# Low parts of 40 weight tiles of layer 1 formed during layer 0, kept in DRAM and loaded

## The chip, the cores and the metric

The program runs on one core of a Trainium2 chip, with TensorE (PE), VectorE (DVE), ScalarE (ACT), GpSimd (POOL) and SyncE (SP), which issues most of the transfers. The metric is the device time of one execution in microseconds (us).

## The reference

A trunk of two layers works on 256 latent and 256 context tokens of width 1024, in fp32. Each layer does the following:

```
h  = rms_norm(x, g) * (1 + scale) + shift            # scale, shift, gates: silu(c) @ w_ada
p  = h @ w_in                                        # one projection, split in columns
A  = bidirectional chunked gated delta rule on q, k, v of p, then norm and silu(z)
B  = b * dwconv3(c * h')                             # short gated convolution
C  = 2-D neighbourhood attention, with all context keys in the same softmax
y  = (gA * (A @ w_pa) + gB * (B @ w_pb) + gC * (C @ w_pc)) @ w_o     # sigmoid gates from p
x += gate1 * y
x += gate2 * ((silu(a) * b) @ w_down),  a, b = dwconv3(h2 @ w_up)
```

Context and latent tokens share the weights. In layer 1 (the last) the context is needed only for keys, values and the delta state, so most projections there have 256 columns instead of 512. The result is the normalized latent stream.

## The kernel before

**Products in three passes.** The matmuls that carry the weights work on operands that are rounded to the fp32r type. To keep fp32 accuracy each operand is held as a high part (the rounded value) and a low part (value minus high part), and `mm3` (L172) adds hi x hi, hi x lo and lo x hi: a tile of 1024 x 128 weights costs 8 x 3 = 24 matmuls. With 512 columns the text calls it a wide tile, with 256 a narrow one.

**Splitting a weight tile.** `wsplit` (L148) loads a tile of 128 x 1024 values (512 KB) on SP's queue into a ring of three raw buffers (tag `wraw`), takes `whi` and `wlo` from rings of three (layer 0) or four (layer 1), casts the raw values into `whi` on ACT (L162) and subtracts on DVE or POOL into `wlo` (L165). Every nth subtraction goes to POOL; n is `LOE`, by stage: in layer 1 every 4th in the delta stage, every 2nd in the rest of the short convolution and z, every 3rd in attention, every 2nd later. A raw buffer is free when the subtraction is done, a `whi` or `wlo` slot when the matmuls of its tile are.

**Order of a layer.** Norm with the first two k tiles and the small a/b projection pipelined into it; then the delta stage: the projections of k, v and q (`gproj`, L509), gram matrices, a substitution of 30 serial steps on DVE (L684 to L688: one product and one addition each), transposes and small matmuls (L735 to L745), and a scan over eight steps into which the matmuls of the short convolution are interleaved (`fill`, L782); the rest of the short convolution, z and the output norm; attention in four head pairs (L978); the merge of the three branches (L1080); w_o; the up projection (22 steps of two tiles, L1174); the down projection (eight tiles of 22 slices, loaded in three pieces, L1203). The modulation vectors of later stages are products on DVE (`ada_all`, L225): each step loads 512 KB into a ring of two and makes one or two passes (L241); `ada_to` spreads 80 steps over layer 0's merge, up and down projection.

**Who sets the order.** The kernel's text gives a program order, and a planner with its own costs places each instruction in its engine's sequence when its inputs and buffers are there in the plan; some matmuls are pinned to program order. On the chip each engine, and SP's and POOL's queues, work through their sequences in order. Temporaries come from rings: `tmp` with tag `tmp` (three) and `tg` (two).

The lines that the change touches:

Of the kernel before, what the change touches and what calls it, by code (L numbers as in the profile page):

```python
# [9 lines left out]
F32 = mybir.dt.float32  # L10
F32R = mybir.dt.float32r
AF = mybir.ActivationFunctionType
ALU = mybir.AluOpType
# [47 lines left out]
PRE = (12, 13, 14, 15, 20, 21)  # L61

ADT = (0, 32, 16, 32)

CTO, CTD = (2, 0), 1
NC0, NUP, HLE = 4, 2, 0
# [15 lines left out]
def trunk(ctx, tc, xin, cin, cbin, con, par, w_ad0, w_ada, w_in, w_ab, bias, w_p, w_o, w_up, w_dn, out, dbg=None):  # L82
# [62 lines left out]

    cb, wsp = [], []

    def wsplit(src, k, m=128, pool=None, bufs=None, dst=None):  # L148
        raw = wraw(src.rearrange("p a b -> p (a b)"), k * m, "wr").rearrange("p (a b) -> p a b", b=m)
        if pool is None:  # L150
            pool, bufs = wsp[0]
        if dst is not None:
            hi, lo = dst
        else:
            hi = pool.tile([P, 8, 128], F32R, tag="whi", bufs=bufs, name="whi")[:, :k, :m]
            lo = pool.tile([P, 8, 128], F32R, tag="wlo", bufs=bufs, name="wlo")[:, :k, :m]
        lo_n[0] += 1
        E_ = G if lo_every[0] and lo_n[0] % lo_every[0] == 0 else V
        na, nb = cuts[0] if k == KD and m == P else (1, 1)
        for i in range(na):  # L160
            c = slice(i * k // na, (i + 1) * k // na)
            A.copy(hi[:, c], raw[:, c])  # L162
        for i in range(nb):
            c = slice(i * k // nb, (i + 1) * k // nb)
            E_.tensor_tensor(lo[:, c], raw[:, c], hi[:, c].bitcast(F32), ALU.subtract)  # L165
        return hi, lo
# [88 lines left out]
    def ada_to(n):  # L255

        if not ada_on:
            ada_on.append(1)
            next(ada_gen)
        while ada_at[0] < n:  # L260
            next(ada_gen)
            ada_at[0] += 1
# [105 lines left out]
    for l in range(L):  # L368
# [15 lines left out]

        adf = {}

        def before(q):
            if l == 0:
                if q == 0:
                    adf[0] = ada_first(0, a0p)  # L390
                    next(adf[0])
                next(adf[q])
                if q == 3:
                    nc.sync.dma_start(cb[0], cbin)
                    A.activation(cb[0], cb[0], AF.Silu)
                if q < 3:
                    adf[q + 1] = ada_first(q + 1, a0p)
                    next(adf[q + 1])
            if q == QW[l]:
                raw = wraw(w_ab[l].rearrange("p a b -> p (a b)"), KD * 16, "wr").rearrange("p (a b) -> p a b", b=16)  # L400
                A.copy(wab[:, :, 0:16], raw)
                V.tensor_tensor(wab[:, :, 16:32], raw, wab[:, :, 0:16].bitcast(F32), ALU.subtract)
                for i in range(NT[l]):
                    pre[GK + i] = wsplit(w_in[l, GK + i], KD)
            if q == QX and l == 0:
                for i in range(NT[l], NT[l] + NPX):
                    pre[PRE[i]] = wsplit(w_in[l, PRE[i]], KD, pool=s0p, bufs=NPX)


        first = {}  # L410
# [55 lines left out]
        def proj(ti, n, name="prj", bank=pbank):  # L466
            if ti in first:
                return first.pop(ti)
            w = pre.pop(ti) if ti in pre else wsplit(w_in[l, ti], KD)
            ps = bank(name)  # L470
            mm3(ps[:, : n.stop - n.start], w, hh, hl, KD, n, True, True)
            return ps
# [279 lines left out]

        def short_conv():
            def fproj(ti):
                hi, lo = wsplit(w_in[l, ti], KD)
                ps = pbank("prj")
                for k in range(KD):
                    for i, (a, b) in enumerate(((hi, hh), (hi, hl), (lo, hh))):
                        mm = PE.matmul(ps[:, OW], a[:, k, :], b[:, k, NA_], start=k == 0 and i == 0, stop=k == KD - 1 and i == 2)  # L759
                        if in_scan[0]:  # L760
                            tc.keep_in_program_order(mm)
                        yield ps
# [214 lines left out]
        with left("at", l) as at:  # L977
            for i in range(4):  # L978
# [23 lines left out]
                if i % 2 == 0:  # L1002
# [3 lines left out]

                    vst = [wp.tile([P, 2, 4, P], F32R, tag="araw", bufs=2, name="vst") for _ in range(2)]
                    for a in range(2):
                        wsplit(w_in[l, NV + i + a], KD, dst=(vh[:, a], vl[:, a]))
                    for b in range(4):  # L1010
                        ps = pbank("pv")
                        n = slice(b * P, b * P + P)
# [67 lines left out]
        for j in range(KD):  # L1080
            acc = tmp("acc")
            for bi, br in enumerate(BRO):
# [12 lines left out]
                    V.tensor_tensor(acc[:, OW], acc[:, OW], gt, ALU.add)  # L1095
                if l == 0:
                    ada_to(ADT[0] + (3 * j + bi + 1) * ADT[1] // 24)
            split(mh[:, j], ml[:, j], acc[:, OW])
        RX.close()

# [50 lines left out]
        with right("f", l) as fp:  # L1151
# [22 lines left out]
            for i in range(FT):  # L1174
# [13 lines left out]
                split(fh[:, i], fl[:, i], uv[0])  # L1188
                if not last:
                    ada_to(sum(ADT[:2]) + (i + 1) * ADT[2] // FT)  # L1190
            cut = 0 if last else CTD
            stat = Stat((fp.tile([P, NW], F32, tag="u", bufs=6, name="sa") if l == 1 else tmp("sa", "tg")), NA_, cut or None)
            norm = None if last else Norm(stat, x, l + 1, "n1g", 1, 0, hh, hl)
# [9 lines left out]
            for j in range(KD):  # L1203
                if j == KD - 1 and cut:
                    ada_to(sum(ADT))
                    w = dsplit(j)
                    last_tiles([j], lambda ps, j, n: dmm(ps, j, n, w), 5, norm)
                    break
# [3 lines left out]
                    mm3(ps[:, OW], w, fh[:, k0 : k0 + kn], fl[:, k0 : k0 + kn], kn, OW, k0 == 0, k0 == 16)  # L1212
                if not last:
                    ada_to(sum(ADT[:3]) + (j + 1) * ADT[3] // KD)
                residual(ps, j, 5, NA_)
                stat.add(x, j)
                if last:
# [139 lines left out]
```

## Time and profile before

| | us |
|---|---|
| median of 3 runs | 1681.98 |
| the runs | 1678.09, 1682.15, 1681.98 |
| the profiled execution | 1677.65 |
| its span, first to last instruction | 1675.9 |
| PE busy in the span | 1593.7 (95%) |
| DVE busy | 1184.9 (71%) |
| ACT busy | 777.9 (46%) |
| POOL busy | 232.3 (14%) |
| mean granted clock of PE | 0.978 |

Matmuls are pipelined, so a PE that counts as busy isn't always at its full rate; the clock column of the windows is the granted share of PE's full clock (1.00 is 2.4 GHz, 0.50 is 1.2 GHz). Times in the rows are from the start of the span. Roughly: layer 0 runs to 1026, with its merge from 420, w_o from 615, up from 661 and down from 903; layer 1's norm and delta stage run to 1228, the rest of its short convolution and z to about 1250, attention to about 1345, then merge, w_o (1445), up (1480) and down (1604).

### The profile page before, as it was taken

The numbers are of one execution on the slowest core, as the hardware profiler recorded it, in microseconds if no ns is written. First come the engines' busy times: TensorE is split into PE (matmuls) and PEld (weight loads), VectorE is DVE, ScalarE is ACT, GpSimd is POOL, SyncE is SP. The second block draws the span as 40 slices with busy tenths as digits, with TensorE's granted clock in tenths as the row PEclk, the third lists the DMA queues.
The fourth block names the chain that finished last, engine by engine and source line by source line (L and its number), as shares of the span: only waits on it lengthen the run. The fifth ranks groups of instructions, "written<-read, shape, count | busy, mean of one in ns | idle before, by whom it ended". The sixth has DMA issues, their size and how long they took to land.

```text
span 1675.9 us, 26346 instructions
## 1 busy us (share of the span) xinstructions
PE 1593.7 (95%) x10184; PEld 1366.0 (82%) x10184; DVE 1184.9 (71%) x2327; ACT 777.9 (46%) x1361; POOL 232.3 (14%) x181
## 2 busy tenths in 40 slices
PE   5999999999799999999999999979999999999997
PEld 4677788887588888888888889668798899989997
DVE  3697753787778776877778667796768755678753
ACT  3764433666322234444443224653356554566653
POOL 0100310100000000000000001212332023334442
PEclk9998999999999999999999999997999999999999
DMA  9221012311556552444445773122033256655663
GB/s 367 76 66 49 26 51 88 120 36 54 196 187 195 171 187 76 136 128 139 126 128 175 252 228 124 51 89 89 26 94 128 60 155 183 189 152 179 187 174 115
DMA packets 65453, 220.04 MB, mean 131 GB/s; under 512 B 7280, under 2 KB 8688, under 8 KB 65200
## 3 DMA queue, kind: packets, MB, share of 16 engines
q1 hardware_dynamic: 64448, 214.20, 40.4%
q0 software_dynamic: 880, 4.16, 0.7%
q8 instruction: 80, 1.31, 0.3%
q14 instruction: 45, 0.37, 0.1%
HBM read 217.28 MB, written 1.05 MB: 130 GB/s over the span
## 4 chain that ended last, share of the span: by engine, by line
PE 79%; DVE 11%; ACT 5%; DMA 2%; issue 2%; POOL 1%; SPq 0%; DVEq 0%; ACTq 0%; POOLq 0%
PE pup L175 7%; PE pup L177 7%; PE pup L176 7%; PE prj L175 6%; PE prj L176 6%; PE prj L177 6%; PE prj L759 5%; PE pdn L176 3%; PE pdn L177 3%; PE pdn L175 3%; PE pa L787 2%; PE pyp L176 2%; PE pyp L177 2%; PE pyp L175 2%; PE po L787 2%
## 5 line engine op out<-in xcount | busy, mean ns | idle before, releaser
L162 ACT CAST whi<-wr 128x1024 fp32r<-128x1024 f32 (+1 forms) x336 | 313.9, 937 | 503.6 <-PE prj L176 147.1
L165 DVE TENSOR_TENSOR wlo<-wr,whi 128x512 fp32r<-128x512 f32 (+2 forms) x340 | 290.1, 871 | 140.8 <-ACT whi L162 138.6
L175 PE MATMUL prj<-hh,whi 128*128 128x512 f32 (+1 forms) x736 | 260.6, 354 | 8.1 <-DVE v__8982 L351 2.5
L177 PE MATMUL prj<-hh,wlo 128*128 128x512 f32 (+1 forms) x736 | 260.9, 355 | 4.9 <-DVE wlo L165 4.9
L176 PE MATMUL prj<-hl,whi 128*128 128x512 f32 (+1 forms) x736 | 259.5, 353 | 0.0
L175 PE MATMUL pup<-hh,whi 128*128 128x256 f32 (+1 forms) x720 | 239.0, 334 | 1.4 <-ACT hh L340 1.4
L176 PE MATMUL pup<-hl,whi 128*128 128x256 f32 (+1 forms) x720 | 238.8, 333 | 0.0
L177 PE MATMUL pup<-hh,wlo 128*128 128x256 f32 (+1 forms) x720 | 238.7, 333 | 0.0
L165 POOL TENSOR_TENSOR wlo<-wr,whi 128x1024 fp32r<-128x1024 f32 (+2 forms) x80 | 163.6, 2046 | 406.5 <-ACT whi L162 392.5
L175 PEld LDWEIGHTS prj<-hh,whi 128*128 128x128 f32 x736 | 140.5, 191 | 28.3 <-DVE v__8982 L351 2.9
L241 DVE SCALAR_TENSOR_TENSOR aprod<-araw,cb 128x1024 bf16<-128x1024 f32 x128 | 153.4, 1220 | 10.7 <-DMA araw<-w_ada 10.4
L177 PEld LDWEIGHTS prj<-hh,wlo 128*128 128x128 f32 x736 | 140.4, 191 | 24.2 <-DVE wlo L165 5.9
L176 PEld LDWEIGHTS prj<-hl,whi 128*128 128x128 f32 x736 | 140.3, 191 | 19.3 <-issue 3.0
L175 PEld LDWEIGHTS pup<-hh,whi 128*128 128x128 f32 x720 | 136.8, 191 | 14.9 <-ACT hh L340 2.0
L177 PEld LDWEIGHTS pup<-hh,wlo 128*128 128x128 f32 x720 | 136.9, 191 | 13.2
L176 PEld LDWEIGHTS pup<-hl,whi 128*128 128x128 f32 x720 | 136.8, 191 | 13.2
L176 PE MATMUL pdn<-fl,whi 128*128 128x256 f32 (+1 forms) x330 | 109.8, 333 | 0.0
L175 PE MATMUL pdn<-fh,whi 128*128 128x256 f32 (+1 forms) x330 | 109.7, 332 | 0.0
L177 PE MATMUL pdn<-fh,wlo 128*128 128x256 f32 (+1 forms) x330 | 109.7, 332 | 0.0
L497 POOL MEMSET wt<- 128x512 f32 x4 | 2.0, 526 | 698.2 <-PE pcut L176 643.9
L350 DVE SCALAR_TENSOR_TENSOR u<-pup,par,u 128x510 f32<-128x510 f32 (+1 forms) x88 | 53.6, 612 | 47.5 <-ACT u L349 47.5
L759 PE MATMUL prj<-hh,whi 128*128 128x512 f32 (+1 forms) x192 | 69.9, 364 | 0.3 <-DVE q__8972 L351 0.3
(346 smaller groups left out, 3213.1 us busy)
## 6 DMA issues: line engine op xcount, KB each, us to landing
wr<-w_in SPq DMA_DIRECT2D x128, 512.0 KB, 3.7
wr<-w_up SPq DMA_DIRECT2D x88, 512.0 KB, 3.6
araw<-w_ada SPq DMA_DIRECT2D x80, 512.0 KB, 4.1
wr<-w_dn SPq DMA_DIRECT2D x32, 512.0 KB, 4.1
wr<-w_p SPq DMA_DIRECT2D x48, 256.0 KB, 2.8
a<-w_ad SPq DMA_DIRECT2D x16, 512.0 KB, 10.4
wr<-w_o SPq DMA_DIRECT2D x16, 512.0 KB, 3.8
wr<-w_dn SPq DMA_DIRECT2D x16, 384.0 KB, 3.5
```

The source lines that it names most:

```text
L162: A.copy(hi[:, c], raw[:, c])
L165: E_.tensor_tensor(lo[:, c], raw[:, c], hi[:, c].bitcast(F32), ALU.subtract)
L175: PE.matmul(ps, hi[:, i, :], xh[:, i, n], start=first and i == 0, stop=False)
L176: PE.matmul(ps, hi[:, i, :], xl[:, i, n], start=False, stop=False)
L177: mm = PE.matmul(ps, lo[:, i, :], xh[:, i, n], start=False, stop=last and i == k - 1)
L241: V.scalar_tensor_tensor(prod, nxt, 1.0, cb[0][:, i], ALU.mult, ALU.mult, accum_out=macc[:, i, b : b + 1])
L350: V.scalar_tensor_tensor(dst[:, :, 1:T], pv[:, :, 0 : T - 1], wc(0), dst[:, :, 1:T], ALU.mult, ALU.add)
L497: G.memset(t, 0.0)
L759: mm = PE.matmul(ps[:, OW], a[:, k, :], b[:, k, NA_], start=k == 0 and i == 0, stop=k == KD - 1 and i == 2)
L787: i_ = PE.matmul(*a, **k)
```

## The change

For 40 of layer 1's 64 projection tiles (all but the 24 gate tiles) the low part is made during layer 0. `lo_all` loads the raw tile on SP into the raw ring, casts half a tile at a time into a temporary on ACT, subtracts it in place on DVE, and POOL issues a store of the result to a DRAM tile. `lo_to` calls this at given points: 12 tiles in the merge, 16 in the up projection, 12 in the down projection (`LDT`), in the order q, k, attention's k, q, the delta's v, attention's v, then short convolution and z (`LOD`). In layer 1 `wsplit` then casts the high part on ACT as before, in one piece, and loads the low part from DRAM on SP's queue straight into its `wlo` slot; there is no subtraction, and the tile isn't counted in the choice between DVE and POOL.

```diff
--- before.py
+++ after.py
@@ -62,6 +62,9 @@
 
 ADT = (0, 32, 16, 32)
 
+LOD = (16, 17, 18, 19, 12, 13, 14, 15, 4, 5, 6, 7, 0, 1, 2, 3, 20, 21, 22, 23, 8, 9, 10, 11) + tuple(range(24, 40))
+LDT = (0, 12, 16, 12)
+
 CTO, CTD = (2, 0), 1
 NC0, NUP, HLE = 4, 2, 0
 SQT, SQ0 = 4, 1
@@ -145,7 +148,30 @@
 
     cb, wsp = [], []
 
-    def wsplit(src, k, m=128, pool=None, bufs=None, dst=None):
+    lod = {}
+
+    def lo_all():
+
+        for ti in LOD:
+            yield
+            raw = wraw(w_in[L - 1, ti].rearrange("p a b -> p (a b)"), KD * P, "lr")
+            for i in range(2):
+                c = slice(512 * i, 512 * i + 512)
+                t = tmp("lh").bitcast(F32R)
+                A.copy(t, raw[:, c])
+                V.tensor_tensor(raw[:, c].bitcast(F32R), raw[:, c], t.bitcast(F32), ALU.subtract)
+            lod[ti] = tc.dram_tile([P, KD * P], F32, name=f"lod{ti}")
+            G.dma_start(lod[ti], raw)
+        yield
+
+    lo_gen, lo_at = lo_all(), [-1]
+
+    def lo_to(n):
+        while lo_at[0] < n:
+            next(lo_gen)
+            lo_at[0] += 1
+
+    def wsplit(src, k, m=128, pool=None, bufs=None, dst=None, lod_=None):
         raw = wraw(src.rearrange("p a b -> p (a b)"), k * m, "wr").rearrange("p (a b) -> p a b", b=m)
         if pool is None:
             pool, bufs = wsp[0]
@@ -154,6 +180,10 @@
         else:
             hi = pool.tile([P, 8, 128], F32R, tag="whi", bufs=bufs, name="whi")[:, :k, :m]
             lo = pool.tile([P, 8, 128], F32R, tag="wlo", bufs=bufs, name="wlo")[:, :k, :m]
+        if lod_ is not None:
+            A.copy(hi, raw)
+            nc.sync.dma_start(lo.bitcast(F32), lod_.rearrange("p (a b) -> p a b", b=m))
+            return hi, lo
         lo_n[0] += 1
         E_ = G if lo_every[0] and lo_n[0] % lo_every[0] == 0 else V
         na, nb = cuts[0] if k == KD and m == P else (1, 1)
@@ -384,6 +414,9 @@
 
         adf = {}
 
+        def win(ti, **a):
+            return wsplit(w_in[l, ti], KD, lod_=lod.get(ti) if last else None, **a)
+
         def before(q):
             if l == 0:
                 if q == 0:
@@ -401,10 +434,10 @@
                 A.copy(wab[:, :, 0:16], raw)
                 V.tensor_tensor(wab[:, :, 16:32], raw, wab[:, :, 0:16].bitcast(F32), ALU.subtract)
                 for i in range(NT[l]):
-                    pre[GK + i] = wsplit(w_in[l, GK + i], KD)
+                    pre[GK + i] = win(GK + i)
             if q == QX and l == 0:
                 for i in range(NT[l], NT[l] + NPX):
-                    pre[PRE[i]] = wsplit(w_in[l, PRE[i]], KD, pool=s0p, bufs=NPX)
+                    pre[PRE[i]] = win(PRE[i], pool=s0p, bufs=NPX)
 
 
         first = {}
@@ -466,7 +499,7 @@
         def proj(ti, n, name="prj", bank=pbank):
             if ti in first:
                 return first.pop(ti)
-            w = pre.pop(ti) if ti in pre else wsplit(w_in[l, ti], KD)
+            w = pre.pop(ti) if ti in pre else win(ti)
             ps = bank(name)
             mm3(ps[:, : n.stop - n.start], w, hh, hl, KD, n, True, True)
             return ps
@@ -752,7 +785,7 @@
 
         def short_conv():
             def fproj(ti):
-                hi, lo = wsplit(w_in[l, ti], KD)
+                hi, lo = win(ti)
                 ps = pbank("prj")
                 for k in range(KD):
                     for i, (a, b) in enumerate(((hi, hh), (hi, hl), (lo, hh))):
@@ -1006,7 +1039,7 @@
 
                     vst = [wp.tile([P, 2, 4, P], F32R, tag="araw", bufs=2, name="vst") for _ in range(2)]
                     for a in range(2):
-                        wsplit(w_in[l, NV + i + a], KD, dst=(vh[:, a], vl[:, a]))
+                        win(NV + i + a, dst=(vh[:, a], vl[:, a]))
                     for b in range(4):
                         ps = pbank("pv")
                         n = slice(b * P, b * P + P)
@@ -1095,6 +1128,7 @@
                     V.tensor_tensor(acc[:, OW], acc[:, OW], gt, ALU.add)
                 if l == 0:
                     ada_to(ADT[0] + (3 * j + bi + 1) * ADT[1] // 24)
+                    lo_to(LDT[0] + (3 * j + bi + 1) * LDT[1] // 24)
             split(mh[:, j], ml[:, j], acc[:, OW])
         RX.close()
 
@@ -1188,6 +1222,7 @@
                 split(fh[:, i], fl[:, i], uv[0])
                 if not last:
                     ada_to(sum(ADT[:2]) + (i + 1) * ADT[2] // FT)
+                    lo_to(sum(LDT[:2]) + (i + 1) * LDT[2] // FT)
             cut = 0 if last else CTD
             stat = Stat((fp.tile([P, NW], F32, tag="u", bufs=6, name="sa") if l == 1 else tmp("sa", "tg")), NA_, cut or None)
             norm = None if last else Norm(stat, x, l + 1, "n1g", 1, 0, hh, hl)
@@ -1203,6 +1238,7 @@
             for j in range(KD):
                 if j == KD - 1 and cut:
                     ada_to(sum(ADT))
+                    lo_to(sum(LDT))
                     w = dsplit(j)
                     last_tiles([j], lambda ps, j, n: dmm(ps, j, n, w), 5, norm)
                     break
@@ -1212,6 +1248,7 @@
                     mm3(ps[:, OW], w, fh[:, k0 : k0 + kn], fl[:, k0 : k0 + kn], kn, OW, k0 == 0, k0 == 16)
                 if not last:
                     ada_to(sum(ADT[:3]) + (j + 1) * ADT[3] // KD)
+                    lo_to(sum(LDT[:3]) + (j + 1) * LDT[3] // KD)
                 residual(ps, j, 5, NA_)
                 stat.add(x, j)
                 if last:
```

## Rows read from the trace of the kernel before

**Rows 1.** The page: busy times, GB/s in 40 slices, the chain's shares.
```profile
PE 1593.7 (95%) x10184; PEld 1366.0 (82%) x10184; DVE 1184.9 (71%) x2327; ACT 777.9 (46%) x1361; POOL 232.3 (14%) x181
...
GB/s 367 76 66 49 26 51 88 120 36 54 196 187 195 171 187 76 136 128 139 126 128 175 252 228 124 51 89 89 26 94 128 60 155 183 189 152 179 187 174 115
...
PE 79%; DVE 11%; ACT 5%; DMA 2%; issue 2%; POOL 1%; SPq 0%; DVEq 0%; ACTq 0%; POOLq 0%
```

**Rows 2.** Busy time by stretch: from:to, us, engines, clock, DMA share, GB/s.
```profile
420.00:615.00 195.00, 184.83 (x791) 150.17 (x792) 152.33 (x265) 59.40 (x87) 0.00 (x0) 0.98 0.59 188
661.00:903.00 242.00, 241.40 (x1112) 201.58 (x1112) 187.81 (x309) 108.30 (x147) 0.00 (x0) 1.00 0.42 128
903.00:1026.00 123.00, 122.04 (x607) 103.78 (x606) 84.31 (x166) 32.25 (x42) 0.00 (x0) 1.00 0.70 223
1026.00:1091.00 65.00, 60.71 (x380) 46.23 (x378) 47.83 (x100) 40.36 (x61) 12.79 (x12) 1.00 0.20 65
1091.00:1148.00 57.00, 41.26 (x316) 36.22 (x317) 53.84 (x112) 27.95 (x42) 11.53 (x5) 0.92 0.35 112
1148.00:1165.00 17.00, 17.00 (x266) 16.36 (x265) 7.74 (x20) 4.69 (x9) 0.00 (x0) 0.50 0.06 16
1165.00:1228.00 63.00, 60.83 (x461) 47.51 (x460) 41.63 (x110) 22.57 (x58) 20.78 (x28) 0.93 0.10 30
```

**Rows 3.** The same for L165 alone.
```profile
1026.00:1091.00 65.00, 7.28 (x6) 4.81 (x2) 1.00 0.20 65
1091.00:1148.00 57.00, 9.76 (x8) 11.38 (x4) 0.92 0.35 112
...
1165.00:1228.00 63.00, 1.85 (x2) 4.76 (x2) 0.93 0.10 30
...
1245.00:1345.00 100.00, 12.66 (x16) 18.67 (x12) 1.00 0.33 101
```

**Rows 4.** What PE waited for, 1091 to 1165: us, times, longest.
```profile
PE pss L535 <- ACT sqk L534: 7.7, 1, 7.7
PE py L739 <- DVE Tl L689: 4.1, 1, 4.1
```

**Rows 5.** Timeline of DVE: start us, us, line, operation.
```profile
1098.69 0.27 DVE L688 TENSOR_TENSOR Bk<-Bk,tm 128x108 f32<-128x108 f32 x1
...
1103.92 1.94 DVE L687 TENSOR_TENSOR tm<-Bk 128x168 f32<-128x168 f32 x1
...
1106.18 0.32 DVE L688 TENSOR_TENSOR Bk<-Bk,tm 128x168 f32<-128x168 f32 x1
...
1141.27 2.50 DVE L688 TENSOR_TENSOR Bk<-Bk,tm 128x108 f32<-128x108 f32 x1
```

**Rows 6.** Timeline of POOL.
```profile
1141.18 2.46 POOL L165 TENSOR_TENSOR wlo<-wr,whi 128x1024 fp32r<-128x1024 f32 x1 [4.20 <-ACT whi L162]
```

**Rows 7.** The chain of waits, 1026 to 1445: start us, us, what.
```profile
1028.77 1.24 DVE wlo L165
1030.65 4.66 PE prj L429 x39
...
1190.50 2.06 DVE wt L805
```

**Rows 8.** DMA issues: queue, count, KB each, median us to landing.
```profile
wr<-w_in SPq DMA_DIRECT2D x128, 512.0 KB, 3.7
...
bt<-bias POOLq DMA_DIRECT2D x8, 384.0 KB, 3.6
```

**Rows 9.** Groups by form: busy us, mean ns, idle before.
```profile
L165 DVE TENSOR_TENSOR wlo<-wr,whi 128x512 fp32r<-128x512 f32 x220 | 145.3, 687 | 63.2 <-ACT whi L162 62.9
...
L162 ACT CAST whi<-wr 128x512 fp32r<-128x512 f32 x80 | 49.3, 621 | 115.9 <-PE prj L176 90.3 <-DMA wr<-w_in 13.8 <-DVE aprod L241 4.4
```

**Rows 10.** What PE waited for, 415 to 1030.
```profile
PE prj L177 <- DVE wlo L165: 4.4, 1, 4.4
```

**Rows 11.** PE's work on prj in a dense narrow run.
```profile
1229.00:1240.00 11.00, 11.00 (x94) 11.00 (x94) 0.42 (x1) 0.35 (x1) 1.00 0.42 130
```

## The prediction

> **What bounds the kernel now.** First the page: TensorE (PE) is counted busy 95% of the span, and 79% of the chain that ended last is PE [rows 1]. That is an average over stages, so the windows come next [rows 2]. In layer 0's merge, up and down projection (420 to 615, 661 to 903, 903 to 1026 us) PE is busy 184.83 of 195, 241.40 of 242 and 122.04 of 123 us, while VectorE (DVE) is at 152.33, 187.81 and 84.31: PE is the limit, and DVE has 43, 54 and 39 us to spare. Layer 1's delta stage is different. Between 1091 and 1148, DVE is busy 53.84 of 57 us and PE 41.26: there DVE sets the pace. It runs the row-by-row substitution (L687, L688) with conv, rope and the low parts of the weights between its steps. The waits say the same: PE stood 7.7 us for the sums of squares, whose input comes through DVE, and 4.1 us for DVE's transpose of the substitution's result [rows 4]. Right after, from 1148 to 1165, the granted clock is 0.50, the 1.2 GHz level [rows 2].
>
> **What the change removes.** Forty of layer 1's splits lose their subtraction, on DVE and on GpSimd (POOL): all of L165 in layer 1's delta and attention stages. The casts on ScalarE (ACT) stay. By stretch [rows 3]: 1026 to 1091 7.28 us on DVE and 4.81 on POOL; 1091 to 1148 9.76 (8 of them, 1.22 each) and 11.38 (4); 1165 to 1228 1.85 and 4.76; 1245 to 1345 12.66 and 18.67.
>
> POOL's part looks free, since nobody on PE waits for it. The timeline of DVE says otherwise [rows 5]: L687 on 168 elements takes 1.94 us at 1103.92, where L688 on the same shape takes 0.32, and L688 on 108 elements takes 2.50 us at 1141.27, where it took 0.27 at 1098.69. At 1141.18 POOL had just begun a 2.46 us subtraction [rows 6], and the long DVE step ends with it. So a DVE step that meets a POOL subtraction can lose some 1.6 to 2.2 us. With four of them in the stretch (first and last shown) I count 4 x 1.9 = 7.7 us.
>
> The Trainium skill (SBUF — State Buffer, section "SBUF: two separate sides") says that DVE and GpSimd share one port pair under an exclusive lock, held for a whole instruction, also by a DVE step with two SBUF inputs against a POOL step that reads SBUF. The trace agrees, 2.50 for 0.27 us. By the rule removing POOL's work gives DVE those 7.7 us; by the view that POOL is off the path, nothing.
>
> **The terms** (minus is gained), against the profiled execution, 1677.65 us, of which the span is 1675.9.
> - *B, 1091 to 1148.* DVE is relieved of 9.8 + 7.7 = 17.5 us, which leaves it about 36. What is late next is PE, busy 41.26 of 57: no more than 15.7 us can go. The substitution's 60 steps are serial and PE's fill work is placed between them, so I take -13; bounds 0 and -16.
> - *A, 1026 to 1091.* 7.28 us leave DVE, which is busy 47.83 of 65. In exchange, the first two low parts can't be loaded before their slots come free at the end of layer 0's last matmuls. Before, the second was subtracted from 1028.77 on, 1.24 us, and PE began at 1030.65 [rows 7]. A load takes 3.7 us to land [rows 8]; issued when the casts run, from 1026 on and two or three at once, it is there between 1030 and 1032 (an estimate). I take -2; bounds -8 and +3.
> - *C, 1148 to 1165.* All 17 us are at the lower clock level, after PE's long waits. If the waits shrink the clock may stay up, and half of 17 us is the most that can go: -2; bounds 0 and -8.
> - *D, the scan, 1165 to 1228.* Two POOL and two DVE subtractions go; one of them meets a DVE step of the scan, 2.06 us on the chain at 1190.50 [rows 7]. The rest is latency between engines: -3; bounds 0 and -7.
> - *E, 1228 to 1345.* Dense PE work and attention, 12.66 us off DVE and 18.67 off POOL, little of it awaited: -1; bounds -6 and +6.
>
> **What it adds in layer 0.** Per low part: one 512 KB load on SP into the ring of three raw buffers, two ACT copies of 0.62 us, two DVE subtractions of 0.69 us [rows 9], one store issued by POOL, which has no other work here. DVE gets 12, 16 and 12 times 1.37 us: 169 of 195, 210 of 242 and 101 of 123 us, still below PE. ACT gets 40 x 1.24 = 50 us over three stages, where it has more to spare. The copies take their slots in the tmp ring of three, beside acc, u and the modulation products. What these delay first is the start of the merge, where PE already stood 4.4 us for a late subtraction on DVE [rows 10].
>
> The raw ring is tightest in the down projection: 123 us for 8 tiles is 15.4 us each, three slots give 46 slot-us. A weight holds one for 3.7 (load) + 1.24 + 1.37 = 6.3 us, three of them 18.9. A low part holds one for 3.7 + 2.6 + its store. No store of this size is in the trace; the nearest row is POOL's bias load of 384 KB, 3.6 us. That makes 9.9, some 13 with queueing (an estimate); 1.5 per tile are 19.5. Sum 38.4 of 46: it fits. The rate there goes from 223 GB/s, 27.4 MB, to 40 MB in 123 us, 325 GB/s; the first slice of the page moved 367 [rows 1]. *F, layer 0:* +4, mostly the merge's start; bounds 0 and +30 (the third rival).
>
> **What it adds in layer 1.** Forty more 512 KB loads on SP, each waiting for its slot, that is for the matmuls of the tile four back. Behind a waiting load stand the next raw loads, and behind those ACT's casts. A narrow tile is 24 matmuls; 94 took 11.00 us [rows 11], so 2.8 us a tile and 8.4 us for the three tiles between. A load needs 3.7: covered, as long as SP issues it in time. In dense narrow runs two loads per 2.8 us are 1.05 MB, 374 GB/s, about the best slice. *G:* +2; bounds 0 and +10.
>
> Against the change speaks the skill's limit of about 358 GB/s from HBM per core (DMA: Bandwidth & Descriptors, section "Specifications"): 1.05 MB then take 2.93 us per narrow tile, 0.13 more than PE. For some 16 such tiles that estimate is 2 us, inside G. The trace had 367 GB/s in a slice of its start.
>
> **Sum:** -13 - 2 - 2 - 3 - 1 + 4 + 2 = -15: 1662.6 for an execution like the profiled one. That one is 4.3 us below the median of the three runs (1681.98) and near their lowest (1678.09), so for the median of new runs I add half of it: 1665.
>
> **Rivals.**
> 1. *More of the same, 1652.* B at PE's limit (-16), clock kept in C (-6), D -6, A and E -4 together, F and G +4: -28, 1649.7 and 1652 for the median. For it: DVE's 95% in B and the 0.50 clock behind it. Against: the substitution is serial, and the order of PE's work is fixed in advance.
> 2. *No change, 1681.* The DVE time that comes free in B is filled by waiting: PE's sequence reaches the sums of squares and L739 no sooner, because gates, loads and projections stand in front. Then B and D give 5, F and G take 6: +1. For it: PE is counted busy 41 of 57 us and can't overtake. Against: both long waits end on DVE work [rows 4].
> 3. *Slower, 1688.* Place: the raw ring in layer 0's down projection. Slots are short from a hold of (46 - 18.9) / 1.5 = 18 us per low part: if the store waits behind DVE's products and lands late, and the hold is 25, a tile needs (18.9 + 37.5) / 3 = 18.8 us in place of 15.4, and 8 tiles cost 27; in place of F's 4; with the other terms (-19) that is +8, and 1688 for the median. For it: SP is one queue in order, so a late raw buffer also holds the modulation loads behind it. Against: the 38 of 46 above.
> 4. *It doesn't do what it says.* If lod were not found, layer 1 would still subtract and the cost alone remain. The dictionary is filled for all 40 before layer 1 begins and every use goes through win, so I give this nothing.
>
> **Chances.** Forecast 0.55, more 0.15, no change 0.16, slower 0.14. 0.3% is 5 us, about what a measurement of this kernel tells from no change. Faster (below 1677) is the forecast and the first rival, 0.70; same 0.16; slower 0.14. The range 1650 to 1685 leaves out most of the third rival and a few hundredths below. The forecast's own range is 1656 to 1675.
>
> **What would show it.** Right: DVE's stretch from Bk's first transpose to its last (L682 to L689) about 13 us shorter, no DVE step of it beyond its usual time, no L165 on POOL before attention ends; PE's 7.7 and 4.1 us waits mostly gone; layer 0's three stages within 4 us. Wrong: PE waits in layer 1 that end on the DMA of a low part, or PE gaps in the down projection that end on whi casts; or B as long as before with DVE idle in it.

## The result, and the profile after

The change makes the kernel slower: 1733.68 us (median of 4, 1731.12 to 1734.04) against 1682.07 for the kernel before, measured beside it, a ratio of 1.032 [1.030, 1.035]. The forecast was 1665. The execution shown here has a span of 1729.4 us, 53.5 more than before.

Stage by stage, each stage counted from the first matmul into its first bank (merge pyp, w_o pwo, up pup, down pdn, layer 1's delta stage pab, attention pl), read from the two traces:

| stage | before | after | difference |
|---|---|---|---|
| layer 0 up to the merge | 420.2 | 422.5 | +2.3 |
| merge | 195.2 | 205.1 | +10.0 |
| w_o | 45.7 | 46.1 | +0.4 |
| up projection | 242.0 | 267.7 | +25.7 |
| down projection and norm | 123.4 | 161.3 | +37.9 |
| layer 1's delta stage | 242.6 | 221.7 | -20.9 |
| the rest of layer 1 | 406.9 | 404.9 | -2.0 |

Layer 1 gives back 23 us, a little more than forecast. The three stages with the added work cost 74, all of layer 0 76. (The stretch ahead of the merge, where only the first low part's load was added, stands between -3.7 and +2.3 in all runs below but e2.) The page after, answering to [rows 1] (busy, GB/s slices, chain, then DMA issues):

```profile
PE 1618.5 (94%) x10184; PEld 1376.1 (80%) x10184; DVE 1185.9 (69%) x2373; ACT 819.0 (47%) x1429; POOL 214.4 (12%) x203
...
GB/s 356 74 74 50 13 62 101 94 38 80 269 220 228 238 222 78 177 193 183 169 193 159 305 286 256 202 133 257 75 105 285 65 119 184 191 151 185 181 180 113
...
PE 61%; DVE 13%; DMA 11%; issue 9%; ACT 5%; POOL 0%; SPq 0%; DVEq 0%; ACTq 0%; POOLq 0%
```

DMA is now 11% of the chain that ended last, where it was 2%, and PE fell from 79% to 61%. DVE's total is as before: 40 low parts are still subtracted, only elsewhere. By stretch, as [rows 2]: merge, up, down, then layer 1 to the substitution, the substitution, to the scan, the scan:

```profile
422.00:628.00 206.00, 189.94 (x794) 152.00 (x794) 164.00 (x285) 69.96 (x110) 5.86 (x11) 0.97 0.68 230
674.00:941.00 267.00, 251.81 (x1110) 204.78 (x1109) 202.98 (x335) 125.97 (x177) 7.97 (x15) 0.96 0.52 172
941.00:1103.00 162.00, 136.21 (x610) 112.01 (x611) 101.99 (x195) 48.20 (x71) 6.95 (x14) 0.89 0.74 261
1103.00:1167.00 64.00, 62.00 (x385) 47.71 (x384) 37.07 (x95) 37.71 (x57) 8.45 (x10) 1.00 0.48 165
1167.00:1206.00 39.00, 37.02 (x302) 33.61 (x301) 35.55 (x101) 27.78 (x42) 0.16 (x1) 1.00 0.74 262
1206.00:1225.00 19.00, 18.14 (x287) 17.32 (x286) 9.12 (x21) 6.96 (x13) 0.00 (x0) 0.60 0.33 108
1225.00:1282.00 57.00, 56.63 (x445) 44.11 (x445) 36.79 (x107) 21.93 (x57) 16.01 (x26) 0.98 0.17 57
```

In the up and down projections no engine fills its stage any more, and the DMA engines stand at 0.52 and 0.74. PE's busy time in the down projection rose from 122.04 to 136.21 us for the same matmuls, with the granted clock at 0.89: after its gaps PE ran part of the stage at the 1.2 GHz level. In the up projection it rose from 241.40 to 251.81 at 0.96, so 10 of the 26 us lost there are a slower PE and the rest gaps. What PE waited for in those stages, 420 to 1103 (before: [rows 10]), and what SP's queue waited for there:

```profile
PE pcut L205 <- ACT whi L192: 7.7, 2, 4.1
PE pdn L205 <- ACT whi L192: 7.5, 5, 2.2
PE pup L205 <- ACT whi L192: 7.2, 6, 1.8
PE stat L332 <- DVE sa L324: 6.1, 1, 6.1
PE pyp L206 <- DVE yl L200: 6.0, 3, 4.6
PE pup L207 <- DVE wlo L195: 6.0, 3, 2.3
...
SPq L138 <- DMA lod<-lr: 72.8, 31, 6.2
```

PE waits mostly for casts and subtractions of the weights, and SP has a wait that was not there before: 31 times it can't issue a load because the raw slot is held by a low part's store that has not landed.

One low part in the up projection (lines of SP, ACT, DVE and POOL from the timeline after):

```profile
762.07 0.38 SPq L138 DMA_DIRECT2D lr<-w_in  x1
...
775.36 0.33 SPq L138 DMA_DIRECT2D lr<-w_in  x1
778.79 0.33 SPq L138 DMA_DIRECT2D wr<-w_up  x1
789.72 0.33 SPq L138 DMA_DIRECT2D wr<-w_up  x1
...
782.70 1.04 ACT L192 CAST whi<-wr 128x1024 fp32r<-128x1024 f32 x1
783.64 0.62 ACT L161 CAST lh<-lr 128x512 fp32r<-128x512 f32 x1
784.76 0.62 ACT L161 CAST lh<-lr 128x512 fp32r<-128x512 f32 x1 [0.50 <-DVE aprod L271]
...
785.30 0.68 DVE L162 TENSOR_TENSOR lr<-lr,lh 128x512 fp32r<-128x512 f32 x1
786.50 0.69 DVE L162 TENSOR_TENSOR lr<-lr,lh 128x512 fp32r<-128x512 f32 x1
787.11 0.69 DVE L195 TENSOR_TENSOR wlo<-wr,whi 128x512 fp32r<-128x512 f32 x1
...
787.49 0.53 POOL L164 DMA_DIRECT2D lod<-lr  x1 [28.09 <-DVE lr L162]
```

Loads, copies and stores of the low parts keep their order, so the copies at 783.64 and 784.76 and the store at 787.49 belong to the load of 762.07. The load of 775.36 is the next low part's; its own store is issued at 798.37. With the 4.0 us that a store takes to land (median of the 40), the slot is held for 29 us. Some 17 of them lie between the load's landing (4.2 us, median) and the first copy, which stands in ACT's order behind the cast at 782.70, of a weight that was itself loaded only at 778.79. From 775.36 on, two of the three slots hold low parts, and the weights go through the third one by one: the load of 789.72 waits for the subtraction of the tile loaded at 778.79. Paired this way, the mean hold is 17.4 us in the merge, 26.0 in the up projection and 18.7 in the down projection, and 51 for the first low part, which is loaded ahead of the merge. The prediction had estimated 13.

### The profile page after: what moved, and what is told of

Read it like the earlier page. It is cut to its first block, busy times and chain, and to the rows that moved or that the text cites. A ratio compares the mean times of both kernels' runs of the same rounds, so it can differ in the third digit from the quotient of the medians.

```text
span 1729.4 us, 26703 instructions
## 1 busy us (share of the span) xinstructions
PE 1618.5 (94%) x10184; PEld 1376.1 (80%) x10184; DVE 1185.9 (69%) x2373; ACT 819.0 (47%) x1429; POOL 214.4 (12%) x203
## 3 DMA queue, kind: packets, MB, share of 16 engines
HBM read 259.22 MB, written 22.02 MB: 163 GB/s over the span
## 4 chain that ended last, share of the span: by engine, by line
PE 61%; DVE 13%; DMA 11%; issue 9%; ACT 5%; POOL 0%; SPq 0%; DVEq 0%; ACTq 0%; POOLq 0%
PE prj L207 6%; PE prj L205 6%; PE prj L206 6%; PE prj L792 5%; PE pup L207 4%; PE pup L205 4%; PE pup L206 4%; DMA lod<-lr 3%; DMA wr<-w_dn 2%; PE pa L820 2%; DVE aprod L271 2%; DVE wlo L195 2%; PE po L820 2%; PE pyp L207 2%; PE pyp L205 2%
## 5 line engine op out<-in xcount | busy, mean ns | idle before, releaser
L192 ACT CAST whi<-wr 128x1024 fp32r<-128x1024 f32 (+2 forms) x292 | 273.8, 941 | 399.5 <-DMA wr<-w_in 79.2
L195 DVE TENSOR_TENSOR wlo<-wr,whi 128x512 fp32r<-128x512 f32 (+2 forms) x310 | 260.7, 860 | 175.9 <-ACT whi L192 170.2
L205 PE MATMUL prj<-hh,whi 128*128 128x512 f32 (+1 forms) x736 | 261.7, 356 | 9.1 <-ACT whi L192 5.1
L205 PE MATMUL pup<-hh,whi 128*128 128x256 f32 (+1 forms) x720 | 242.6, 339 | 8.6 <-ACT whi L192 7.2
L195 POOL TENSOR_TENSOR wlo<-wr,whi 128x1024 fp32r<-128x1024 f32 (+2 forms) x66 | 132.2, 2002 | 322.4 <-ACT whi L192 317.8
L271 DVE SCALAR_TENSOR_TENSOR aprod<-araw,cb 128x1024 bf16<-128x1024 f32 x128 | 153.1, 1219 | 10.0 <-DMA araw<-w_ada 9.9
L207 PEld LDWEIGHTS pup<-hh,wlo 128*128 128x128 f32 x720 | 138.3, 193 | 22.9 <-DVE wlo L195 9.4
L164 POOL DMA_DIRECT2D lod<-lr x40 | 21.3, 532 | 677.0 <-DVE lr L162 677.0
L161 ACT CAST lh<-lr 128x512 fp32r<-128x512 f32 x80 | 48.4, 618 | 68.7 <-DVE aprod L271 52.5
```

What stands on the lines that cost most here:

```text
L161: A.copy(t, raw[:, c])
L164: G.dma_start(lod[ti], raw)
L205: PE.matmul(ps, hi[:, i, :], xh[:, i, n], start=first and i == 0, stop=False)
L207: mm = PE.matmul(ps, lo[:, i, :], xh[:, i, n], start=False, stop=last and i == k - 1)
L271: V.scalar_tensor_tensor(prod, nxt, 1.0, cb[0][:, i], ALU.mult, ALU.mult, accum_out=macc[:, i, b : b + 1])
```

## The experiments

H1: a low part holds one of three raw slots until its store lands, and the weights' loads come late. H2: its copies and subtractions stand ahead of the weights' casts and subtractions in ACT's and DVE's order. H3: the added DMA traffic slows the weights. Stage differences below are against the trace of before, in us:

| run | ratio | merge | up | down | delta stage of layer 1 |
|---|---|---|---|---|---|
| the change | 1.032 [1.030, 1.035] | +10.0 | +25.7 | +37.9 | -20.9 |
| e1 layer 1 only | 0.985 [0.978, 0.992] | +0.9 | 0.0 | +0.8 | -24.5 |
| e2 copies in DRAM | 1.016 [1.009, 1.022] | +1.8 | 0.0 | +2.2 | -21.8 |
| e3 no engine work | 1.000 [0.997, 1.002] | +0.6 | +1.4 | +24.1 | -20.8 |
| e4 no stores | 1.007 [1.004, 1.010] | +4.3 | +12.6 | +22.0 | -20.6 |
| e5 layer 0 only | 1.042 [1.039, 1.046] | +10.8 | +25.6 | +38.5 | +1.4 |
| e6 POOL forms them | 1.042 [1.037, 1.048] | +22.7 | +23.7 | +52.0 | -22.9 |
| e7 other ring | 1.047 [1.038, 1.055] | +15.1 | 0.0 | +86.9 | -23.0 |
| e8 first 28 tiles | 1.021 [1.015, 1.027] | +11.7 | +26.0 | +6.4 | -1.9 |
| e9 16 tiles, up, other ring | 0.987 [0.984, 0.990] | +0.2 | 0.0 | +0.3 | -21.6 |
| e10 24 tiles | 1.000 [0.998, 1.001] | +1.7 | +11.8 | +10.8 | -22.9 |
| e11 40 tiles | 1.083 [1.079, 1.087] | +0.1 | +101.2 | +67.9 | -24.5 |
| e12 12 tiles, merge | 1.001 [0.999, 1.003] | +11.5 | +1.4 | 0.0 | -13.4 |
| e13 copies in DRAM, in place | 0.992 [0.987, 0.997] | +0.1 | 0.0 | +8.0 | -20.5 |
| e14 as e9, raw ring, SP | 1.005 [1.004, 1.007] | +0.7 | +25.6 | +6.8 | -20.6 |
| e15 as e9, SP's queue | 0.989 [0.982, 0.996] | +0.2 | 0.0 | +2.5 | -20.6 |
| e16 as e9, raw ring | 1.004 [1.002, 1.007] | +0.1 | +25.8 | +7.8 | -21.8 |
| e17 e3, even in down | 0.995 [0.991, 0.999] | +2.4 | +1.4 | +13.8 | -21.7 |
| e18 change, even in down | 1.024 [1.021, 1.027] | +12.9 | +25.2 | +28.4 | -22.3 |

### The two sides: e1, e5

```diff
 e1, in lo_all: only the first tile is formed and stored
-            lod[ti] = tc.dram_tile(...); G.dma_start(lod[ti], raw)
+            lod[ti] = one_        # the one tile
 e5, in win
-            lod_=lod.get(ti) if last else None
+            lod_=None
```

> Only layer 1's part of the change: one low part is formed and stored in layer 0, and layer 1 loads that one tile 40 times, so the low parts' values of 39 tiles are wrong. Theory (layer 0 pays about 75 us for forming the parts, layer 1 gains about 20): 1660, between 1655 and 1666. Rival (layer 1's gain seen between the two traces is owed to something that layer 0 left behind, such as weights loaded earlier): within 5 of the kernel before, 1677 to 1687.

> Layer 0 forms and stores the 40 low parts as in the change, layer 1 ignores them and subtracts as before. If the change is the sum of its two sides (layer 0's three stages 74 us longer, layer 1 24 shorter): 1753 to 1760. Rival (part of what layer 0 loses is given back or made up by what layer 1 does): 1735 to 1748.

Measured 1655.1 and 1754.9. The two sides add: layer 1's part alone is worth 24 us, layer 0's alone costs 72 (1754.9 - 1683.0), and the sum of their stage differences is the change's. So nothing of the loss shows in layer 1's loads.

### What in layer 0: e2, e3, e4, e13

```diff
 e2, in lo_all                                  (e3: load and store; e4: no store)
-            raw = wraw(...); copies, subtractions; G.dma_start(lod[ti], raw)
+            G.dma_start(lod[ti], w_in[L - 1, ti])
 e13: in two halves, each behind a small store of the modulation accumulators
+                G.dma_start(lod[ti][:, c.start : c.start + 8], macc[:, 0])
+                G.dma_start(lod[ti][:, c], w_in[L - 1, ti][:, c])
```

> Layer 0's 40 steps only copy the raw tile inside DRAM (one DMA each on POOL's queue): no raw slot, no copies on ACT, no subtractions on DVE, but the same 20 MB read and 20 MB written; the values of the low parts are wrong. Theory H1 (a low part holds one of three raw slots until its store lands) and theory H2 (its copies and subtractions stand ahead of the weights' casts and subtractions in the engines' order): 1660 to 1668. Theory H3 (the added DMA traffic itself slows the weights' loads): 1715 to 1735.

> Layer 0's 40 steps load the raw tile into the raw ring and store it at once: no copies, no subtractions; the values are wrong. H1: the slot is held for load and store, about 9 of the 16 us seen, so a third to a half of layer 0's 75 us stays: 1685 to 1700. H2: the engines' work is gone and so is the cost: 1660 to 1668. H3: nothing changes, 1720 to 1735.

> Layer 0's 40 steps load the tile, copy and subtract as before, but only the first is stored, and layer 1 loads that one; the values are wrong. H1: the slot comes free some 5 us sooner of 16, so about two thirds of the 75 stay: 1700 to 1715. H2: the engines' work is all there, 1725 to 1735. H3: half of the traffic is gone, 1690 to 1700.

> As e2, a copy of the raw tile inside DRAM in place of each of the 40 low parts (the values are wrong), but each copy now has to wait for the modulation accumulators of its step, so that it runs where the change runs its step; in two halves of 128 x 512. The same 20 MB read and 20 MB written, no slot, nothing on SP, ACT and DVE. H1 (slots, and SP's order behind them): layer 0 within 5 of before, 1655 to 1664. H3 (the traffic): the down projection alone 15 to 24 longer, as in e3, 1672 to 1685.

e2 missed its purpose: with nothing to wait for, POOL issued all 40 copies in the first 125 us of the program, and the merge began 48 us later. Its later stages are unhurt. e13 put the copies where the change has its steps: merge and up as before, down 8 longer (1664.7, just above H1's range). So the traffic of 20 MB in and out costs at most those 8 us, and none before the down projection's last tile. The first seven tiles of e13 took 104.7 us by their first matmuls, as before, and PE was full, as this row of its windows shows:

```profile
903.00:1007.00 104.00, 104.00 (x461) 86.11 (x460) 66.45 (x128) 25.46 (x30) 21.38 (x40) 1.00 0.82 273
```

H3 is out, but for the last tile. The Trainium skill (DMA: Bandwidth & Descriptors, section "Specifications") sets some 358 GB/s per core as HBM's limit, and the 273 here with PE full agrees that the limit was not met. The 273 counts a byte copied inside DRAM once (e13's page has 262.34 MB of packets, and 259.22 MB read from HBM and 22.35 written); with the copies counted twice it is some 325, an estimate, and still below.

e3 measured 1679.4 and e4 1692.1; neither lies in a range that H1 or H2 had named. Without the engines' work (e3) the hold falls to 9.0, 8.4 and 9.8 us in the three stages, and merge and up are free. Without the stores (e4) it is 15.9, 21.8 and 16.6, and merge and up lose about half of what the change loses. In the up projection the cost goes with the hold, and not in proportion: 1.4 us at 8.4, 12.6 at 21.8, 25.7 at 26.0. The slots give the scale: three slots over 242 us are 726 slot-us; 16 holds of 26.0 take 416 and leave 7.0 for each of the 44 weight tiles; the stage became 267.7 us, which is 8.8 for each.

### Other engines, other rings, fewer tiles: e6, e7, e8, e12

```diff
 e6, in lo_all
-                A.copy(t, raw[:, c]);  V.tensor_tensor(raw[:, c] ...)
+                G.tensor_copy(t, raw[:, c]);  G.tensor_tensor(raw[:, c] ...)
 e7
-            raw = wraw(...)                                        # ring of 3, on SP
+            raw = wp.tile(..., tag="araw", bufs=2); G.dma_start(raw, ...)  # and araw's loads on G
 e8:  LOD = the first 24 of the list + (24, 25, 26, 27);  LDT = (0, 12, 16, 0)
 e12: LOD = (24 .. 35);  LDT = (0, 12, 0, 0)
```

> The whole change, but the cast and the subtraction of a low part in layer 0 are both done by POOL, which is idle there; ACT and DVE issue nothing for the low parts. H1 with the queues (the raw slot is held so long because the casts wait behind ACT's and the subtractions behind DVE's own work, and nothing of ACT's or DVE's waits on it any more): layer 0's 74 us fall to 30 to 45, mostly in the down projection, 1688 to 1705. Rival (POOL's subtractions lengthen DVE's steps in layer 0 as they do in layer 1, 1 to 2 us each, and hold the slot as long): 1725 or more.

> The whole change, but layer 0's raw tile for a low part lies in the two-slot ring of the modulation weights, and that ring's loads are issued from POOL's queue: the raw ring of three and SP's queue then carry only the projections' weights. H1 (the raw ring and the SP queue behind it): merge and up come back to within 5 us of the kernel before, down within 25: 1675 to 1695. H2 (copies and subtractions ahead of the weights' in ACT's and DVE's order): 1715 to 1735. Rival to both (the ring of two now holds up the modulation steps on DVE, and DVE the subtractions of the weights): above 1735.

> 28 low parts (the first 24 of the list and the first 4 of the third branch's) are formed, 12 in the merge and 16 in the up projection as in the change, none in the down projection. If each stage's loss is its own: merge 10 and up 26 longer as in the change, down within 3 of before; layer 1 gains 14 to 22 with 28 of 40 tiles: 1696 to 1706. Rival (the down projection is late from what up left behind): 1710 to 1725.

> 12 low parts (tiles 24 to 35) in the merge, through the raw ring as in the change, none in up and down. Merge 10 longer as in the change, layer 1 gains 12 to 20: 1670 to 1680. Rival (12 tiles give little, as the first 28 did): 1686 to 1694.

e6 (1755.3) is slower than the change. POOL needs 924 + 1597 ns for what ACT and DVE do in 618 + 686, and the slot is held a little longer (19.5, 27.9, 20.2 us), though nothing of the low parts stands in ACT's or DVE's order any more. That the up projection still loses 23.7 us speaks against H2 there. From the lines of e6, 420 to 1123 (the change has 1219 ns for the product on DVE):

```profile
L271 DVE SCALAR_TENSOR_TENSOR aprod<-araw,cb 128x1024 bf16<-128x1024 f32 x128 | 173.8, 1371 | 30.2 <-DMA araw<-w_ada 20.6 <-POOL lr L162 9.4
L162 POOL TENSOR_TENSOR lr<-lr,lh 128x512 fp32r<-128x512 f32 x80 | 127.5, 1597 | 5.0
L161 POOL CAST lh<-lr 128x512 fp32r<-128x512 f32 x80 | 73.8, 924 | 490.1 <-DVE aprod L271 439.1 <-DMA lr<-w_in 46.7 <-issue 2.4
```

The last line is the one to read. POOL, with little else to do, mostly waits not for the low part's load but for a modulation product on DVE (`aprod`), from which the copy needs nothing but the temporary's slot: both take theirs from the `tmp` ring of three. So a second short ring stretches the hold in the first. In the change, ACT stood 52.5 us before the copies for the same products over the kernel: 26.6 in the merge, 4.4 in the up projection, 21.5 in the down projection. No run gave the copies a ring of their own.

The Trainium skill (Perfetto Trace Analysis, section "Optimizing Scalar/DVE Operations") says that offloading DVE's work to GpSimd may make sense, but reminds that the two share an SBUF read port, so that it might not help; here 0.15 us on each of 128 products, 20 us of DVE, agrees, though no run shows that the port is the reason.

e7 (1762.7) was worse in sum, but its stages settle something: in the up projection the same 16 low parts cost 0.0. In the merge and above all in the down projection, where 32 modulation tiles go through the two slots of this ring in each stage, they cost 15 and 87. So for the merge no run shows that the raw ring is the cost.

e8 (1719.7) was a surprise: merge and up lost as expected, and the down projection, without a low part, 6.4 us where at most 3 had been expected. All of it is in its first of eight tiles (21.5 us instead of 15.0), which the change has too (21.7): the up projection's delay reaches into it. Layer 1 gained 1.9 us with 28 of 40 tiles, not 14 to 22. The substitution took 48.9 us instead of 55.9, but the scan gave the gain back: from its first to its last matmul (pa) 71 us, where before had 60, at a granted clock of 0.83. Why the scan is slower there is not shown: between the substitution and the scan's last matmul lie five subtractions of weights, where before has four. e12 (1682.3, between its two ranges), with tiles 24 to 35 in the merge, gained 13.4 and paid 11.5, so the tiles used during and right behind the substitution seem to carry the gain.

### The ring or the queue: e9, e14, e15, e16, and the ring's limit: e10, e11

```diff
 all four: 16 tiles, formed in the up projection only
+LOD = tuple(range(16, 20)) + tuple(range(24, 36));  LDT = (0, 0, 16, 0)
 e9
-            raw = wraw(...)
+            raw = wp.tile([P, 1024], F32, tag="araw", bufs=2, name="lr")
+            G.dma_start(raw, ...)         # in up, araw's own loads on G too
 e14: wraw, SP (as the change)    e15: "araw", SP    e16: "wraw", G
 e10: as e9 with tiles 12 to 35, 24 steps    e11: as e9 with all 40, 40 steps
```

> 16 low parts only (tiles 16 to 19 and 24 to 35 of layer 1's projections, used in the delta stage), all formed in layer 0's up projection, in the ring of the modulation weights; in the up projection both of that ring's loads come from POOL's queue, elsewhere the modulation loads stay on SP. Theory (a low part in the raw ring was the cost in the up projection, its copies and subtractions are free there): up within 3 of before, merge and down as before, layer 1 gains 14 to 22: 1660 to 1669. Rival 1 (the copies and subtractions cost 10 or more in up when only the ring is changed): 1672 to 1682. Rival 2 (16 tiles aren't enough, the scan gives back what the substitution gained, as with the first 28): 1675 to 1685.

> The 16 low parts of e9 in the up projection, but as in the change: raw ring, loads on SP. Up 26 longer as in the change (16 there too), layer 1 as e9: 1680 to 1690. Rival (e9 was faster only for having its low parts in one stage): 1658 to 1666.

> As e9, in the ring of the modulation weights, but with that ring's loads on SP's queue in the up projection too. If the raw ring alone is the cost: 1657 to 1663. If SP's queue is (its next weight stands behind a load that waits for its slot): up 10 to 26 longer, 1668 to 1686.

> As e9, but the low parts in the raw ring of three, their loads and the modulation loads issued from POOL's queue in the up projection. If the raw ring is the cost: up 15 to 30 longer, 1674 to 1690. If SP's queue alone is: 1657 to 1663.

> The same with the 24 tiles 12 to 35. Theory: up is 0 to 8 longer with 24 low parts and 16 modulation tiles through two slots, layer 1 gains 18 to 24: 1657 to 1668. Rival (a ring of two is too short for 40 tiles in 242 us): up 15 or more longer, 1670 to 1685.

> The same with all 40 tiles of the change. 56 tiles through two slots in 242 us leave 8.6 us for each hold; the low part needs 4 to load, 4 to store and 3 or more between. Theory: up 30 to 60 longer, layer 1 gains 24: 1688 to 1720. Rival (the ring is no bound, copies and subtractions are free): 1660 to 1668.

In the raw ring the up projection is 25.6 and 25.8 us longer, whichever queue loads the low parts; in the modulation weights' ring it is 0.0 and 0.0. The same 32 copies and 32 subtractions run in all four. (In e16 the modulation loads stayed on SP's queue, unlike what was written ahead of it.) So H1 stands for this stage, and SP's queue has no part in it. The holds: 26.0 and 25.6 us in the raw ring, 10.7 and 10.6 in the other. The engines' order is not the same in the four, since the planner makes it anew: in e14 and e16, as in the change, three to five casts of weights stand between a low part's load and its first copy (18 us on average), in e9 and e15 at most one (some 4.5 us). From the windows of e9 and of e16, the up projection:

```profile
661.00:903.00 242.00, 241.40 (x1114) 201.62 (x1114) 202.78 (x334) 121.57 (x174) 22.83 (x43) 1.00 0.58 187
```

```profile
661.00:929.00 268.00, 252.55 (x1112) 205.48 (x1113) 203.93 (x337) 126.57 (x177) 16.56 (x31) 0.96 0.52 172
```

DVE and ACT do as much in both; PE has no gap in the first. What PE waits for in e16 there is what it waits for after the change:

```profile
PE pup L206 <- ACT whi L193: 7.1, 6, 1.8
PE pup L208 <- DVE wlo L196: 6.0, 3, 2.3
```

A low part in the up projection of e9, from its timeline:

```profile
744.76 0.53 POOL L158 DMA_DIRECT2D lr<-w_in  x1 [0.92 <-DVE aprod L272]
752.11 0.54 POOL L165 DMA_DIRECT2D lod<-lr  x1 [6.82 <-DVE lr L163]
...
749.87 1.14 ACT L162 CAST lh<-lr 128x512 fp32r<-128x512 f32 x2 [2.07 <-DMA lr<-w_in]
...
750.52 1.29 DVE L163 TENSOR_TENSOR lr<-lr,lh 128x512 fp32r<-128x512 f32 x2 [1.73 <-ACT lh L162]
```

ACT waits for the low part's load and not for a weight's, and the store is issued 7.4 us after the load instead of 25.4. The first line says why: here the load itself waits until a modulation product has freed its slot, and the copies can follow as soon as it lands. In the raw ring the load is issued early and waits in the slot for its place in ACT's order. How much of that place is owed to the `tmp` slot, to the planner and to late weights was not separated; raw ring and early copies together were not tried. e9 is faster than both kernels, 1658.14 us, 1.3% below before (0.987 [0.984, 0.990]).

e10 (1680.8) and e11 (1821.2) show the limit of two slots. 24 low parts and 16 modulation tiles lose 12 us in up and 11 in down, into which the last steps slip, in the rival's range; all 40 lose 101 and 68. The 30 to 60 expected of e11 were too low for the up projection alone, and 9 of its low parts were still loaded in the down projection, which the estimate had left out.

### The down projection: e17, e18

25 of the 38 us are lost in the last two of its eight tiles: the first six took 103.1 us instead of 89.7, the seventh 31.7 instead of 15.0, the last 26.4 instead of 18.6 (first matmuls of pdn and pcut). From the windows after, tiles seven and eight:

```profile
1045.00:1103.00 58.00, 40.91 (x214) 35.63 (x213) 34.70 (x70) 15.86 (x28) 2.70 (x6) 0.79 0.64 222
```

```diff
 e18 (e17: the same on e3)
-                    lo_to(sum(LDT[:3]) + (j + 1) * LDT[3] // KD)
+                    lo_to(sum(LDT[:3]) + min(j + 1, 6) * LDT[3] // 6)
```

> As e3 (load and store only, values wrong), but the 12 steps of the down projection lie in its first six tiles, two a tile, none in the last two. Theory (the loss of e3 is the last two tiles' own: two low parts and the modulation tiles are issued there ahead of the last weights): the down projection is 3 to 10 longer than before instead of 24, 1658 to 1667. Rival (the ring is short wherever the low parts lie): the loss moves to the first six tiles, 1672 to 1682.

> The whole change with the down projection's 12 steps in its first six tiles. Theory (last two tiles' bunching is 20 of the 38): 1708 to 1718. Rival (with a hold of 18.7 us the ring is short throughout, 12 x 18.7 + 24 x 8.8 slot-us in three slots make 145 us instead of 123, and two low parts a tile only move the loss): 1722 to 1735.

Neither came as the theory had it: e17 (1674.0) lies in the rival's range and e18 (1721.9) at its lower edge. Moving the steps forward takes 10 us off in each (38 to 28, 24 to 14), so the last steps' bunching costs 10. Some 7 are the first tile's, left over from the up projection (e8, e14 and e16 have them without a low part in this stage). e13's 8 us in the last tile need no slot.

The count of slots does not give the rest. Here the cost doesn't go with the hold: 24.1 us at 9.8 (e3), 22.0 at 16.6 (e4). In e18 the hold fell to 13.3 us; 12 of them and 24 weight tiles at the up projection's 8.8 make 371 slot-us, 124 us in three slots, no more than the stage had, yet it took 151.7. SP's queue still stood 38 us there for stores of low parts to land, in 9 waits, so single late slots in front of an ordered queue may be the cause. Ring and queue were not told apart in this stage as they were in the up projection, and its cause stays open in part.

## Why the prediction was wrong, point by point

- **The step that failed is F**, put as "+4, mostly the merge's start; bounds 0 and +30". It measured +74 in the three stages (10 + 26 + 38), 2.5 times its upper bound. Three things in it were wrong. The hold of a low part was taken as the sum of its own steps, "9.9, some 13 with queueing"; it was 17 to 26, because the copies wait with the loaded tile for their place in ACT's order and for a slot of the `tmp` ring behind a modulation product. The prediction had named that ring, and expected its delay first at the merge's start. The slot arithmetic was made for the down projection alone; for the merge and the up projection none was worked out, though up had 16 low parts and lost 26. And the point from which slots are short, 18 us, came from 6.3 us per weight; the up projection shows 8.8, with which three weights take 26.4 of the 46 slot-us and the point is 13 us. The estimate of 13 stood right on that edge. In the up projection the runs show the step's failure and its cause; in the merge and the down projection they show its size, and leave its cause open in part.
- **The third rival** had the right place and mechanism (the raw ring, stores that land late), a chance of 0.14 and a price of 27 in down. Down alone cost 38, 7 of them left over from up, and two more stages lost time too. What it said for itself, that SP is one queue in order, had no weight in the up projection (e14, e16).
- **B, -13:** right, and larger. From L682 to L689 before took 55.9 us (1089.46 to 1145.33), and after, L715 to L722, 39.1: -16.8, a little past the bound of -16 that PE's busy time had set. From the timelines before (two lines) and after:

```profile
1089.46 2.00 DVE L682 STREAM_TRANSPOSE Bk<-Tl 128x1024 f32<-128x1024 f32 x1
...
1145.33 1.91 DVE L689 STREAM_TRANSPOSE Tl<-Bk 128x1024 f32<-128x1024 f32 x1
...
1166.72 2.10 DVE L715 STREAM_TRANSPOSE Bk<-Tl 128x1024 f32<-128x1024 f32 x1
...
1205.82 2.03 DVE L722 STREAM_TRANSPOSE Tl<-Bk 128x1024 f32<-128x1024 f32 x1
```

No subtraction of a weight is left in the stretch on DVE or POOL, and none of the Bk steps that took about 2 us [rows 5] does so any more. PE became the limit, 37.02 of 39 us. Against [rows 4], the waits of 7.7 and 4.1 shrank to:

```profile
PE pss L568 <- ACT sqk L567: 1.5, 1, 1.5
...
PE py L772 <- DVE Tl L722: 0.9, 1, 0.9
```

- **A, -2:** +0.9 (first pab to L682: 63.0 and 63.9), inside its bounds. **C, -2:** -2.3 (L689 to the first pa), the clock at 0.60 for 0.50 [rows 2]. **D, -3:** -4.4 (the scan's first pa to the end of its last po). **E, -1:** -0.1. **G, +2:** -0.3 from the second merge on; PE waits on a low part's load once, 2.5 us in attention. The sum of layer 1 was forecast at -19 and measured -23.
- **What would have shown it:** "layer 0's three stages within 4 us" is the line that failed, and the PE gaps that end on whi casts are there as the prediction described them under "Wrong".

## What to carry to other kernels

Moving work from a stage bound by DVE to one bound by PE is right only if the buffers there are free, not just the engines: count slot-us for every stage that receives work, with the hold taken from the issue of the load to the landing of the store and with the wait for every other ring and in-order engine in it. A load that is issued long before its copies can run holds its slot for nothing. The count is a test for shortage, not a price: it fitted the up projection and missed the down projection. Move as little as carries the gain (16 of 40 tiles did) and put it in a ring whose own users can wait.

## What the runs showed of the hardware that was not expected

A copy inside DRAM of 512 KB, issued as 16 x 8192 elements at the program's start, took a median of 13.7 us to land, and the first loads beside it took 22.6 where e1 has 10.3. From e2's DMA issues:

```profile
lod<-w_in POOLq DMA_DIRECT2D x40, 512.0 KB, 13.7
...
a<-w_ad SPq DMA_DIRECT2D x16, 512.0 KB, 22.6
```

The same bytes as halves of 128 x 512 elements, beside the projections in e13, landed in 4.7 us each.
